# Interleaving the first loads of a fused attention block, storing its own features by unit, reordering its norm statistics, and loading its latent weights in column blocks

## The chip, the cores and the metric

The kernel runs on all 8 NeuronCores of one Trainium2 chip; the cores do not talk to each other. The metric is the device time of one execution, taken on the slowest core. Executions come in two states: in the slow one a die runs at a lower granted TensorE clock and the time is longer. Everything below compares fast executions. A profile shows one fast execution; its page is about the slowest core of that execution, so the pages of two kernels may show different cores.

## The reference, cut to what matters

```python
h = rms_norm(x, g_in)                                   # x: (2, 4096, 2048)
(c_q, c_kv, k_pe, z_mla, q_swa, k_swa, v_swa, z_swa, q_mem, z_mem) = split_cols(h @ w_in, IN_SIZES)
y_mla = mla_attention(c_q, c_kv, k_pe, ...)   # per head: q from w_uq, k and v from w_ukv; block-causal
y_swa = swa_attention(q_swa, k_swa, v_swa, ...)         # window, sinks
y_mem = memory_attention(q_mem, rms_norm(mem), ...)
y = concat([y_mla, y_swa, y_mem] * silu(gates)) @ w_out
return rms_norm(x + y, norm_final)
```

Four cores share one sequence. Each core owns 1,024 of its 4,096 tokens: it computes queries, gates and outputs for those, but compressed keys and values for all 4,096.

## The kernel before

A core's tokens come as 8 **units** of 512. Units 0 and 1 are its own tokens and stay in the buffer `hown`; units 2 to 7 pass through four rotating buffers `hrot`. Features come transposed (2,048 features in 16 chunks of 128 rows, named `kc`) as f32 in memory, and are cast to bf16 by the load; in this kernel the loads that cast go on GpSimd's queue ("pool", below the *software queue*). The weights of the units go on SyncE's queue ("sp", the *hardware queue*). For each unit TensorE forms five column groups (two of latent, one of rotary key, one of key, one of value) from the weights `wkv`. These arrive as f32 in four quarters (`wst`), and VectorE multiplies the norm gain in (*fold*) while it writes `wkv`. So a quarter of unit 0's work needs one quarter of features and one folded quarter of weights.

```python
hown = P.sb("hown", [128, 16, 1024], BF16, 34 * KB)       # [row, kc, own token]: a unit's row is cut in 1 KB runs

def load_x(i):                                            # i = half unit
    hb, ap = xhalf(i)
    n = 8 // len(hb)
    for k, b_ in enumerate(hb):
        P.dma("pool", ap[:, k * n:(k + 1) * n, :], xu_d[i]..., b_, writes=[b_])

for q in range(3):
    load_kv(q)                                            # "sp": wst[q] <- weights, f32
for i in range(4):
    load_x(i)                                             # "pool": hown <- features, f32 to bf16
...
for q in range(4):
    fold_kv(q)                                            # VectorE: wkv[q] = wst[q] * gain
    if q == 0:
        load_kv(3); load_cs(0); ...                       # first buffer free again; rotary table; identity
    ...
    stat_sq(q // 2, q % 2)                                # ScalarE: squares of the features
    for g, b in ((0, 0), (1, 1), (3, KB_), (4, VB), (2, GB)):
        group(0, g, b, 4 * q, 4 * q + 4)                  # TensorE
```

The RMS norm is applied late: ScalarE squares the features, VectorE adds the squares up (`stat_add`, into `qt`), and TensorE sums over rows with a matrix of ones (`stat_m`); the result scales what is read out of PSUM.

```python
    kpe_r(0)                          # unit 0's read-out, while TensorE is in unit 1
    kpe(0, GB)                        # three VectorE steps of the rotary key
    lat_n(0, 0)                       # two more
    stat_add(2)                       # unit 1: the first half's sum of squares
    ...
    else:                             # units 2 to 7
        ... groups 0, 1
        if u < 4: group(u, 3, KB_)
        stat_m(u)
        group(u, 2, GB)
    ...
    if u < 4:
        swa_k(u, KB_)                 # VectorE reads the key bank out
    ...
        lat_m(u, 6)
        if u > 1: group(u, 4, VB)
    if u == 3:                        # first own query product, into the key bank
        proj(wb, wp, 0, KB_)
```

After the units come the products of own tokens with streamed weights (`stage`, f32, 512 KB halves on the hardware queue; folded into `ring` by VectorE or GpSimd): query latents, memory keys and values, and 16 **gate** columns `z`. In the middle of the gates the weights of the latent stage are fetched, as two loads with a cast:

```python
        if kind == "z" and c == 3:
            P.dma("pool", wuq.t[:].rearrange("p a b -> p (a b)"), wuq_d[:, :], wuq, writes=[wuq])      # 2 MB as bf16
            P.dma("pool", wukv.t[:].rearrange("p a b -> p (a b)"), wukv_d[:, :], wukv, writes=[wukv])  # 1 MB
```

Then come the latent attention over 8 heads, and the output projection.

Of the kernel before, what the change touches and what calls it, by code (L numbers as in the profile page):

```python
# [164 lines left out]
def build():  # L165
# [32 lines left out]
    def pf(b, c0, c1, p0=0, p1=128):  # L198
        o = (b % 2) * 512
        return DB[b // 2][p0:p1, o + c0:o + c1]  # L200
# [26 lines left out]
    vv = P.sb("vv", [128, 16, 128], BF16, 30 * KB)  # L227
    hown = P.sb("hown", [128, 16, 1024], BF16, 34 * KB)
    hownp = [[P.part(hown) for _ in range(4)] for _ in range(2)]
    hrot = [P.sb("hrot", [128, 8, 512], BF16, (74 + 8 * i) * KB) for i in range(4)]  # L230
# [25 lines left out]

    def xhalf(i):

        u, kh = i // 2, i % 2
        if u < 2:  # L260
            n = len(hownp[u]) // 2
            return hownp[u][kh * n:(kh + 1) * n], hown.t[:, kh * 8:(kh + 1) * 8, u * 512:(u + 1) * 512]
        b = hrot[(i - 4) % 4]
        return [b], b.t[:, :, :]

    def hpart(u, kc):
        b, ap = xhalf(2 * u + kc // 8)
        return ap[:, kc % 8, :]

    def hbufs(u):  # L270
        return xhalf(2 * u)[0] + xhalf(2 * u + 1)[0]

    def load_x(i):
        hb, ap = xhalf(i)
        n = 8 // len(hb)
        for k, b_ in enumerate(hb):
            P.dma("pool", ap[:, k * n:(k + 1) * n, :],
                  xu_d[i].rearrange("p (a b) -> p a b", b=512)[:, k * n:(k + 1) * n, :], b_, writes=[b_])

# [3 lines left out]

    def stat_sq(i, k=None):

        hb, ap = xhalf(i)
        for j in (range(2) if k is None else (k,)):
            ks = slice(4 * j, 4 * j + 4)
            act(AF.Square, sqb.t[:, ks, :], ap[:, ks, :], [hb[j % len(hb)]], [sqp[j]])

# [14 lines left out]
    def stat_m(u):  # L305
        rb, r_, eb, e_ = r_of(u)

        def mm(e):
            for c in range(4):
                ins = e.matmul(pf(6, 0, 512), lhsT=ones.t[:], rhs=qt.t[:, c, :], start=(c == 0), stop=(c == 3))  # L310
            return ins
        P.op("pe", mm, reads=[ones, qt], writes=[PS[6]])
        act(AF.Ln, r_, pf(6, 0, 512), [PS[6]], [rb], bias=EPS, scale=1.0 / D)
        P.op("dve", lambda e: e.tensor_scalar(out=e_, in0=pf(6, 0, 512), scalar1=EPS / D, scalar2=EPS * EPS,
                                              op0=ALU.mult, op1=ALU.add), reads=[PS[6]], writes=[eb])
        act(AF.Exp, r_, r_, [rb], [rb], scale=-0.5)

    def group(u, g, b, k0=0, k1=16):


        bufs = hownp[u][k0 // 4:k1 // 4] if u < 2 else hbufs(u)

        def mm(e):
            for kc in range(k0, k1):
                if g < 4:
                    ins = e.matmul(pf(b, 0, 512), lhsT=wkv.t[:, kc, g * 128:(g + 1) * 128], rhs=hpart(u, kc),  # L326
                                   start=(kc == 0), stop=(kc == 15))
                    continue
                for t in range(4):
                    ins = e.matmul(pf(b, t * 128, (t + 1) * 128), lhsT=hpart(u, kc)[:, t * 128:(t + 1) * 128],  # L330
                                   rhs=wkv.t[:, kc, 512:640], start=(kc == 0 and t == 0), stop=(kc == 15),
                                   skip_group_check=True)
            return ins
        P.op("pe", mm, reads=wkvp[k0 // 4:k1 // 4] + bufs, writes=[PS[b]])

# [56 lines left out]

    def load_kv(q):
        w_ = wst[q % 3]
        P.dma("sp", w_.t[:].rearrange("p a b -> p (a b)"), wkv_d[q], w_, writes=[w_])

    def fold_kv(q):
        tt(ALU.mult, wkv.t[:, 4 * q:4 * q + 4, :], wst[q % 3].t[:], g_in[:, 4 * q:4 * q + 4].unsqueeze(2).to_broadcast(
            [128, 4, 640]), [wst[q % 3], gv], [wkvp[q]])

    for q in range(3):
        load_kv(q)
    for i in range(4):
        load_x(i)

# [54 lines left out]
    def proj(wb, wp, hf, b):  # L460
        def mm(e):
            for kc in range(16):
                ins = e.matmul(pf(b, 0, 512), lhsT=wb.t[:, kc, :], rhs=hown.t[:, kc, hf * 512:(hf + 1) * 512],  # L463
                               start=(kc == 0), stop=(kc == 15))
            return ins
        P.op("pe", mm, reads=wp + hownp[hf], writes=[PS[b]])
# [34 lines left out]
    for q in range(4):  # L501
        fold_kv(q)
        if q == 0:
            load_kv(3)
            load_cs(0)
            P.dma("sp", ident.t[:], idn_d[:, :], ident, writes=[ident])
        if q == 2:
            stat_add(0)
        stat_sq(q // 2, q % 2)
        for g, b in ((0, 0), (1, 1), (3, KB_), (4, VB), (2, GB)):  # L510
            group(0, g, b, 4 * q, 4 * q + 4)
            if q == 3 and g == 1:
                lat_sq(0)
    stat_add(1)
    stage.extend(P.sb("stage", [128, 8, 128], F32, (166 + 4 * i) * KB) for i in range(4))
# [3 lines left out]
    for u in (2, 3):  # L519
        load_x(2 * u)  # L520
        load_x(2 * u + 1)
        load_cs(u, "pool")
# [7 lines left out]

    stat_sq(2, 0)
    stat_m(0)
    stat_sq(2, 1)
    for q in range(2):
# [5 lines left out]
    lat_t(0, 6)  # L540
    kpe_r(0)
    kpe(0, GB)
    lat_n(0, 0)
    stat_add(2)
    stat_sq(3, 0)
    for g in range(2):
        group(1, g, 2 + g, 8, 12)
    for g, b in ((3, KB_), (4, VB), (2, GB)):
        group(1, g, b, 0, 12)
    stat_sq(3, 1)  # L550
    stat_add(3)
    load_cs(5)
    for u in range(1, 8):
        p0 = 2 * (u % 2)
        if u == 1:
            stat_m(u)
            for g in range(2):
                group(1, g, 2 + g, 12, 16)
            lat_sq(p0)
            for g, b in ((3, KB_), (4, VB), (2, GB)):  # L560
                group(1, g, b, 12, 16)
        else:
            for k in range(2):
                for g in range(2):
                    group(u, g, p0 + g, 8 * k, 8 * k + 8)
            lat_sq(p0)
            if u < 4:
                group(u, 3, KB_)
            stat_m(u)
            group(u, 2, GB)  # L570
        if u < 7:
            stat_sq(2 * u + 2)
        kpe_r(u)
# [5 lines left out]
        if u < 4:  # L579
            lat_m(u, 6)  # L580
            if u > 1:
                group(u, 4, VB)
            lat_t(u, 6)
            lat_n(u, p0)
# [19 lines left out]
        if u < 7:  # L604
            stat_sq(2 * u + 3)
            stat_add(2 * u + 3)
# [5 lines left out]
        if 1 < u < 6:  # L612
            load_x(2 * u + 4)
            load_x(2 * u + 5)
        if u == 6:
# [225 lines left out]
    for kind, c in chunks:  # L841
# [80 lines left out]
        if kind == "z" and c == 3:  # L922
            assert not side
            wuq = P.sb("wuq", [128, 4, 2048], BF16, 126 * KB)
            wukv = P.sb("wukv", [128, 2, 2048], BF16, 142 * KB)
            P.dma("pool", wuq.t[:].rearrange("p a b -> p (a b)"), wuq_d[:, :], wuq, writes=[wuq])
            P.dma("pool", wukv.t[:].rearrange("p a b -> p (a b)"), wukv_d[:, :], wukv, writes=[wukv])
            P.dma("pool", kpeT.t[64:128, :], kpeT.t[0:64, :], kpeT, reads=[kpeT], writes=[kpeT])
# [416 lines left out]
```

## Time and profile before

| | |
|---|---|
| time, median of fast runs | 820.48 us |
| TensorE busy / idle on the slowest core | 750.6 / 68.4 us |
| first matmul | 26.25 us |
| next two TensorE waits (64 and 84 us) | 3.67 and 2.47 us |
| TensorE waits among the gates (375 to 393 us) | 3.34, 0.96, 1.56 us |

The head of the page, slowest core: engine, busy time, share of the span, instructions.

```profile
span 819.0 us, 12755 instructions; the slowest of 8 cores (806.6 to 819.0 us)
...
PE 750.6 (92%) x4463; PEld 361.9 (44%) x4463; DVE 544.8 (67%) x792; ACT 424.7 (52%) x539; POOL 100.6 (12%) x82
```

TensorE waits for little, so a change can win only from its idle 68 us and from the slower matmuls after a gap (after the 3.67 us wait at 64 us, seven begin 420 to 427 ns after the one before, not 216; see below). The waits view of TensorE (line that waited, what it waited for, total us, times, longest us):

```profile
PE psd L326 <- DMA hown_57<-xu: 26.3, 1, 26.3
PE psd L310 <- DVE qt_64 L206: 6.1, 2, 3.7
PE psd L463 <- DVE zrt_114 L206: 4.9, 2, 3.3
...
PE psd L463 <- DVE zrt_113 L206: 1.0, 1, 1.0
```

The longest of them is before the first matmul. The timeline of the start shows how it comes about (columns: start, duration, engine, line, operation, output <- inputs, forms; in brackets the idle time of the engine before it and what ended it):

```profile
1.49 0.42 SPq L147 DMA_DIRECT2D wst_77<-wkv  x1
1.58 6.10 POOL L147 DMA_DIRECT2D hown_57<-xu  x8 [0.33 <-issue]
...
9.77 2.83 DVE L206 TENSOR_TENSOR wkv_62<-wst_77,gv_44 128x2560 bf16<-128x2560 f32 x1 [9.77 <-DMA wst_77<-wkv]
...
20.67 2.83 DVE L206 TENSOR_TENSOR wkv_62<-wst_79,gv_44 128x2560 bf16<-128x2560 f32 x1 [2.47 <-DMA wst_79<-wkv]
...
26.25 4.92 PE L326 MATMUL psd<-hown_57,wkv_62 128*128 128x512 bf16 x12 [26.25 <-DMA hown_57<-xu]
```

Both queues got their orders by 7.7 us. Three weight quarters land and are folded (from 9.8, 15.4 and 20.7 us on) while the first quarter of features, ordered at 1.58 us, lands only at 26.1 us. The records of DMA packets show why. In the stretch from 8 to 22 us they hold 349 weight packets of 10,240 B and 386 feature packets of 1,024 B: the counts are nearly equal, so the queue with pieces a tenth as long moved about a tenth of the other's bytes (0.40 against 3.57 MB). That the queues took turns piece by piece is inferred from the counts, since the records do not name the engine: on this core, when the first 48 feature pieces had begun, so had 31 weight pieces beyond the first quarter's 128. Spread evenly over the 16 engines, that is three pieces an engine of the one and two of the other, which long turns would not give.

The second wait, in unit 1:

```profile
56.16 1.22 DVE L206 TENSOR_TENSOR qt_64<-sqb_63 128x2048 bf16<-128x2048 bf16 x1
57.46 3.71 ACT L203 ACTIVATE sqb_63<-hown_57 128x2048 bf16<-128x2048 bf16 x2 [4.19 <-DVE qt_64 L206]
...
63.98 1.07 PE L310 MATMUL psd<-qt_64,ones_43 128*128 128x512 bf16 x4 [3.67 <-DVE qt_64 L206]
...
84.30 1.02 PE L310 MATMUL psd<-qt_64,ones_43 128*128 128x512 bf16 x4 [2.47 <-DVE qt_64 L206]
```

VectorE adds unit 1's first squares only after unit 0's rotary key and latents; ScalarE sat idle 4.19 us because the buffer of squares was not free; so the last sum was ready at 63.8 us and TensorE waited 3.67 us. The last line is the like wait in unit 2.

The waits among the gates:

```profile
376.11 1.23 DVE L206 TENSOR_TENSOR ring_87<-stage_83,gv_44 128x1024 bf16<-128x1024 f32 x1 [6.02 <-DMA stage_83<-wti]
...
378.08 8.75 PE L463 MATMUL psd<-hown_57,ring_86 128*128 128x512 bf16 x32 [3.34 <-DVE zrt_114 L206]
...
385.82 1.23 DVE L206 TENSOR_TENSOR ring_84<-stage_81,gv_44 128x1024 bf16<-128x1024 f32 x1 [4.13 <-DMA stage_81<-wti]
...
387.80 3.61 PE L463 MATMUL psd<-hown_57,ring_87 128*128 128x512 bf16 x16 [0.96 <-DVE zrt_113 L206]
...
392.97 3.61 PE L463 MATMUL psd<-hown_57,ring_87 128*128 128x512 bf16 x16 [1.56 <-DVE zrt_114 L206]
```

TensorE waits for VectorE, but VectorE had itself waited 6.02 and 4.13 us for stages, whose landing took up to 27.4 us in this stretch, beside the latent weights' pieces of 16,384 B (`wuq`) and 8,192 B (`wukv`). Note also that the 32 matmuls at 378 us took 8.75 us, about 1.7 us more than without a gap, since nine of them begin 305 to 427 ns after the one before, not 216; the trace's record of the granted clock has one half for 3.41 us from 378.84 us on. The same record has one half for 3.41 us after each of the two waits of the statistics matmul (from 64.82 and 85.30 us).

### The profile page before, as it was taken

The numbers are of one execution on the slowest core, as the hardware profiler recorded it, in microseconds if no ns is written. First come the engines' busy times: TensorE is split into PE (matmuls) and PEld (weight loads), VectorE is DVE, ScalarE is ACT, GpSimd is POOL, SyncE is SP. The second block draws the span as 40 slices with busy tenths as digits, with TensorE's granted clock in tenths as the row PEclk, the third lists the DMA queues.
The fourth block names the chain that finished last, engine by engine and source line by source line (L and its number), as shares of the span: only waits on it lengthen the run. The fifth ranks groups of instructions, "written<-read, shape, count | busy, mean of one in ns | idle before, by whom it ended". The sixth has DMA issues, their size and how long they took to land.

```text
span 819.0 us, 12755 instructions; the slowest of 8 cores (806.6 to 819.0 us)
## 1 busy us (share of the span) xinstructions
PE 750.6 (92%) x4463; PEld 361.9 (44%) x4463; DVE 544.8 (67%) x792; ACT 424.7 (52%) x539; POOL 100.6 (12%) x82
## 2 busy tenths in 40 slices
PE   0798899998789999997998999999999998999995
PEld 0353454444333454443444555545545453444442
DVE  2445676776686766764955888888888887256334
ACT  0455545554453337763545767677676775332222
POOL 5100000002232332221210110101101010000000
PEclk9999999999999999999999999999999999999998
DMA  8999489877464585489310616100101189209313
GB/s 230 196 165 218 108 168 168 172 185 197 126 155 128 147 230 144 124 153 233 103 33 0 128 30 103 28 11 17 26 2 27 35 192 217 99 1 289 122 52 103
DMA packets 24895, 99.62 MB, mean 122 GB/s; under 512 B 2750, under 2 KB 7102, under 8 KB 20544
## 3 DMA queue, kind: packets, MB, share of 16 engines
q1 hardware_dynamic: 16544, 64.58, 26.7%
q0 software_dynamic: 8288, 34.22, 25.0%
q8 instruction: 37, 0.61, 0.3%
q14 instruction: 26, 0.21, 0.1%
HBM read 115.18 MB, written 8.39 MB: 151 GB/s over the span
## 4 chain that ended last, share of the span: by engine, by line
PE 75%; DVE 11%; DMA 6%; ACT 4%; issue 4%; DVEq 0%; ACTq 0%; POOL 0%; SPq 0%; POOLq 0%
PE psd L463 19%; PE psd L1107 13%; PE psd L326 10%; PE psd L997 6%; PE psd L1029 5%; PE psd L983 4%; PE psd L831 3%; DMA hown_57<-xu 3%; DMA stage_81<-wti 3%; PE psd L817 2%; PE psd L792 2%; PE psd L330 1%; PE psd L848 1%; PE psd L310 1%; DVE pac_147 L206 1%
## 5 line engine op out<-in xcount | busy, mean ns | idle before, releaser
L463 PE MATMUL psd<-hown_57,ring_85 128*128 128x512 bf16 x288 | 64.5, 379 | 2.1 <-ACT sqq_94 L203 2.1
L326 PE MATMUL psd<-hown_57,wkv_62 128*128 128x512 bf16 x128 | 33.1, 415 | 26.3 <-DMA hown_57<-xu 26.3
L463 PE MATMUL psd<-hown_57,ring_87 128*128 128x512 bf16 x224 | 51.9, 386 | 2.5 <-DVE zrt_114 L206 1.6
L463 PE MATMUL psd<-hown_57,ring_84 128*128 128x512 bf16 x224 | 50.5, 382 | 0.0
L463 PEld LDWEIGHTS psd<-hown_57,ring_85 128*128 128x128 bf16 x288 | 27.7, 98 | 37.2 <-issue 4.6
L997 PE MATMUL psd<-Qn_122,Kb_129 128*128 128x512 bf16 (+2 forms) x192 | 43.3, 328 | 0.0
L997 PE MATMUL psd<-Qn_121,Kb_128 128*128 128x512 bf16 (+2 forms) x192 | 43.2, 328 | 0.0
L463 PE MATMUL psd<-hown_57,ring_86 128*128 128x512 bf16 x160 | 37.5, 392 | 3.3 <-DVE zrt_114 L206 3.3
L203 ACT ACTIVATE pmb_132<-psd 128x1024 bf16<-128x1024 f32 x24 | 24.6, 1024 | 26.1 <-PE psd L997 26.1
L831 PEld LDWEIGHTS psd<-wukv_120,kvnT_53 128*128 128x128 bf16 x512 | 31.5, 99 | 10.9 <-issue 7.0
L203 ACT ACTIVATE pmb_136<-psd 128x1024 bf16<-128x1024 f32 x24 | 24.5, 1021 | 22.6 <-PE psd L997 22.5
L831 PE MATMUL psd<-wukv_120,kvnT_53 128*128 128x128 bf16 x512 | 34.6, 222 | 1.4 <-ACT Kb_128 L203 1.4
L463 PEld LDWEIGHTS psd<-hown_57,ring_87 128*128 128x128 bf16 x224 | 21.8, 99 | 31.1 <-issue 6.8
L817 PE MATMUL psd<-kvnT_53,wukv_120 128*128 128x512 bf16 x128 | 33.7, 386 | 0.8 <-DVE Vb_130 L216 0.8
L463 PEld LDWEIGHTS psd<-hown_57,ring_84 128*128 128x128 bf16 x224 | 21.9, 99 | 27.3 <-issue 2.0
L326 PEld LDWEIGHTS psd<-hown_57,wkv_62 128*128 128x128 bf16 x128 | 13.1, 105 | 42.5 <-issue 31.2
L792 PE MATMUL psd<-cqT_90,wuq_119 128*128 128x512 bf16 x128 | 30.2, 379 | 0.0
L203 ACT ACTIVATE pmb_134<-psd 128x1024 bf16<-128x1024 f32 x24 | 24.6, 1024 | 7.3 <-PE psd L997 6.1
L203 ACT ACTIVATE pmb_137<-psd 128x1024 bf16<-128x1024 f32 x24 | 24.4, 1018 | 6.0 <-PE psd L997 6.0
L203 ACT ACTIVATE pmb_135<-psd 128x1024 bf16<-128x1024 f32 x24 | 24.5, 1021 | 5.4 <-PE psd L997 5.4
L463 PEld LDWEIGHTS psd<-hown_57,ring_86 128*128 128x128 bf16 x160 | 16.0, 100 | 23.7 <-issue 6.1
L203 ACT ACTIVATE r2t_72<-r2t_72 128x512 f32<-128x512 f32 x16 | 10.1, 630 | 29.5 <-DVE r2t_72 L209 28.7
(402 smaller groups left out, 1649.0 us busy)
## 6 DMA issues: line engine op xcount, KB each, us to landing
stage_82<-wti SPq DMA_DIRECT2D x15, 512.0 KB, 7.2
stage_83<-wti SPq DMA_DIRECT2D x15, 512.0 KB, 6.6
stage_80<-wti SPq DMA_DIRECT2D x11, 512.0 KB, 6.6
stage_81<-wti SPq DMA_DIRECT2D x11, 512.0 KB, 6.3
hown_57<-xu POOLq DMA_DIRECT2D x8, 512.0 KB, 33.6
tq_151<-tq_126 SPq DMA_DIRECT2D x14, 256.0 KB, 3.4
hrot_58<-xu POOLq DMA_DIRECT2D x3, 1024.0 KB, 11.1
hrot_59<-xu POOLq DMA_DIRECT2D x3, 1024.0 KB, 18.8
```

The costliest lines, as they stand in the source:

```text
L203: P.op("act", lambda e: e.activation(out=out, in_=in_, func=func, **kw), reads=reads, writes=writes)
L206: P.op(eng, lambda e: e.tensor_tensor(out=out, in0=a, in1=b, op=op), reads=reads, writes=writes)
L310: ins = e.matmul(pf(6, 0, 512), lhsT=ones.t[:], rhs=qt.t[:, c, :], start=(c == 0), stop=(c == 3))
L326: ins = e.matmul(pf(b, 0, 512), lhsT=wkv.t[:, kc, g * 128:(g + 1) * 128], rhs=hpart(u, kc), start=(kc == 0), stop=(kc == 15))
L463: ins = e.matmul(pf(b, 0, 512), lhsT=wb.t[:, kc, :], rhs=hown.t[:, kc, hf * 512:(hf + 1) * 512], start=(kc == 0), stop=(kc == 15))
L792: ins = e.matmul(pf(2 * k + hf, 0, 512), lhsT=wuq.t[:, kc, col:col + 128], rhs=cqT.t[:, kc, hf * 512:(hf + 1) * 512], start=(kc == 0), sto ...
L817: ins = e.matmul(pf(2 * k + t, 0, 512), lhsT=wukv.t[:, kc, h * 256:h * 256 + 128], rhs=kvnT.t[:, kc, (2 * c + t) * 512:(2 * c + t + 1) * 512],
L831: ins = e.matmul(pf(2 * k + t // 4, (t % 4) * 128, (t % 4 + 1) * 128), lhsT=kvnT.t[:, kc, tl * 128:(tl + 1) * 128], rhs=wukv.t[:, kc, h * ...
L983: ins = e.matmul(pf(2 * k + t, c0, c1), lhsT=kpeT.t[rows, tile * 128:(tile + 1) * 128], rhs=Qp[s].t[rows, q0 + qc:q0 + qc + c1 - c0], star ...
L997: ins = e.matmul(pf(2 * k + t, c0, c1), lhsT=Kb[s].t[:, tile * 128:(tile + 1) * 128], rhs=Qn[s].t[:, q0 + qc:q0 + qc + c1 - c0], start=Fal ...
L1029: ins = e.matmul(pf(ob, qc, qc + c1 - c0), lhsT=Vb[s].t[:, tile, :], rhs=pb.t[:, t, c0:c1], start=(st["first"] and i == 0), stop=(lst and ...
L1107: ins = e.matmul(pf(b, 0, 512), lhsT=gate(kc)[:, tt_ * 128:(tt_ + 1) * 128], rhs=wo[ci].t[:, kc, :], start=(kc == 0), stop=(kc == 15))
```

## The change

It has four parts. (1) Weight quarters 1 to 3 move to the software queue, alternating with the quarters of unit 0's features, in order of use; weight quarter 0 stays on the hardware queue, and the rotary table and the identity now follow it at once; the last feature quarter is cut in two. (2) `hown` is stored by unit, so that a feature quarter is one 4 KB run per row instead of four of 1 KB. (3) The order of statistics and latent-norm steps in units 0 to 3 changes. (4) The latent weights come in blocks of 512 columns: eight loads of 1 KB runs instead of one of 16 KB runs (`wuq`) and one of 8 KB runs (`wukv`).

```diff
-    hown = P.sb("hown", [128, 16, 1024], BF16, 34 * KB)
+    hown = P.sb("hown", [128, 2, 16, 512], BF16, 34 * KB)
+    cuts = [(0, 4, 8, 12, 14, 16), (0, 4, 8, 12, 16)]
 ...
+    load_kv(0, "sp")
+    load_cs(0)
+    P.dma("sp", ident.t[:], idn_d[:, :], ident, writes=[ident])
     for q in range(3):
-        load_kv(q)
-    for i in range(4):
-        load_x(i)
+        load_xk(0, 4 * q, 4 * q + 4)
+        if q < 2:
+            load_kv(q + 1)                # now on "pool"
 ...
         if q == 0:
             load_kv(3)
-            load_cs(0)
-            P.dma("sp", ident.t[:], idn_d[:, :], ident, writes=[ident])
+            load_xk(0, 12, 14)
+            load_xk(0, 14, 16)
+            load_x(1)
 ...
     kpe_r(0)
+    stat_add(2)
     kpe(0, GB)
     lat_n(0, 0)
-    stat_add(2)
 ...
             if u < 4:
                 group(u, 3, KB_)
-            stat_m(u)
-            group(u, 2, GB)
+                group(u, 2, GB)
+                stat_m(u)
+            else:
+                stat_m(u)
+                group(u, 2, GB)
 ...
-            lat_m(u, 6)
             if u > 1:
                 group(u, 4, VB)
+            lat_m(u, 6)
 ...
-            P.dma("pool", wuq.t[:]..., wuq_d[:, :], wuq, writes=[wuq])
-            P.dma("pool", wukv.t[:]..., wukv_d[:, :], wukv, writes=[wukv])
+            for w_, d_ in ((wuq, wuq_d), (wukv, wukv_d)):
+                for c_ in range(4):
+                    cs_ = slice(c_ * 512, (c_ + 1) * 512)
+                    P.dma("pool", w_.t[:, :, cs_], d_.rearrange("p (a b) -> p a b", b=2048)[:, :, cs_], w_, writes=[w_])
```

Besides, unit 0's squares are summed in another way (four more ones-matmuls instead of a VectorE addition), and the squares of unit 1's first quarter are taken after unit 0's statistics matmul.

More of the change, by code (lines that the diff above doesn't have):

```diff
@@ L227, in build @@
     vv = P.sb("vv", [128, 16, 128], BF16, 30 * KB)
-    hown = P.sb("hown", [128, 16, 1024], BF16, 34 * KB)
-    hownp = [[P.part(hown) for _ in range(4)] for _ in range(2)]
+    hown = P.sb("hown", [128, 2, 16, 512], BF16, 34 * KB)
+    cuts = [(0, 4, 8, 12, 14, 16), (0, 4, 8, 12, 16)]
+    hownp = [[P.part(hown) for _ in c_[1:]] for c_ in cuts]
     hrot = [P.sb("hrot", [128, 8, 512], BF16, (74 + 8 * i) * KB) for i in range(4)]
@@ L255, in build, with fparts, feats, load_xk @@
     OUTS = [P.mk(None), P.mk(None)]
-    def xhalf(i):
-        u, kh = i // 2, i % 2
+    def fparts(u, k0, k1):
         if u < 2:
-            n = len(hownp[u]) // 2
-            return hownp[u][kh * n:(kh + 1) * n], hown.t[:, kh * 8:(kh + 1) * 8, u * 512:(u + 1) * 512]
-        b = hrot[(i - 4) % 4]
-        return [b], b.t[:, :, :]
-    def hpart(u, kc):
-        b, ap = xhalf(2 * u + kc // 8)
-        return ap[:, kc % 8, :]
-    def hbufs(u):
-        return xhalf(2 * u)[0] + xhalf(2 * u + 1)[0]
-    def load_x(i):
-        hb, ap = xhalf(i)
-        n = 8 // len(hb)
-        for k, b_ in enumerate(hb):
-            P.dma("pool", ap[:, k * n:(k + 1) * n, :],
-                  xu_d[i].rearrange("p (a b) -> p a b", b=512)[:, k * n:(k + 1) * n, :], b_, writes=[b_])
+            return [b_ for b_, c0, c1 in zip(hownp[u], cuts[u], cuts[u][1:]) if c0 < k1 and k0 < c1]
+        return [hrot[(2 * u + kh) % 4] for kh in range(2) if 8 * kh < k1 and k0 < 8 * kh + 8]
+    def feats(u, k0, k1):
+        if u < 2:
+            return hown.t[:, u, k0:k1, :]
+        return hrot[(2 * u + k0 // 8) % 4].t[:, k0 % 8:k0 % 8 + k1 - k0, :]
+    def hpart(u, kc):
+        return feats(u, kc, kc + 1)[:, 0, :]
+    def load_xk(u, k0, k1):
+        (b_,) = fparts(u, k0, k1)
+        i, j = 2 * u + k0 // 8, (k0 % 8) * 512
+        P.dma("pool", feats(u, k0, k1).rearrange("p a b -> p (a b)"), xu_d[i][:, j:j + (k1 - k0) * 512], b_, writes=[b_])
+    def load_x(u):
+        for k0, k1 in zip(cuts[u], cuts[u][1:]) if u < 2 else ((0, 8), (8, 16)):
+            load_xk(u, k0, k1)
     def load_cs(u, q="sp"):
@@ L282, in load_cs, with stat_sq @@
         P.dma(q, c_.t[:], csk_d[u], c_, writes=[c_])
-    def stat_sq(i, k=None):
-        hb, ap = xhalf(i)
-        for j in (range(2) if k is None else (k,)):
-            ks = slice(4 * j, 4 * j + 4)
-            act(AF.Square, sqb.t[:, ks, :], ap[:, ks, :], [hb[j % len(hb)]], [sqp[j]])
+    def stat_sq(u, k0, k1):
+        for a0 in range(k0, k1, min(4, k1 - k0)):
+            a1 = min(a0 + 4, k1)
+            act(AF.Square, sqb.t[:, a0 % 8:a0 % 8 + a1 - a0, :], feats(u, a0, a1), fparts(u, a0, a1), [sqp[a0 % 8 // 4]])
     def stat_add(i):
@@ L306, in stat_m @@
         rb, r_, eb, e_ = r_of(u)
+        parts = [qt.t[:, c, :] for c in range(4)] + ([sqb.t[:, c, :] for c in range(4, 8)] if u == 0 else [])
         def mm(e):
-            for c in range(4):
-                ins = e.matmul(pf(6, 0, 512), lhsT=ones.t[:], rhs=qt.t[:, c, :], start=(c == 0), stop=(c == 3))
+            for i, a_ in enumerate(parts):
+                ins = e.matmul(pf(6, 0, 512), lhsT=ones.t[:], rhs=a_, start=(i == 0), stop=(i == len(parts) - 1))
             return ins
-        P.op("pe", mm, reads=[ones, qt], writes=[PS[6]])
+        P.op("pe", mm, reads=[ones, qt] + ([sqp[1]] if u == 0 else []), writes=[PS[6]])
         act(AF.Ln, r_, pf(6, 0, 512), [PS[6]], [rb], bias=EPS, scale=1.0 / D)
@@ L318, in group @@
     def group(u, g, b, k0=0, k1=16):
-        bufs = hownp[u][k0 // 4:k1 // 4] if u < 2 else hbufs(u)
+        bufs = fparts(u, k0, k1)
         def mm(e):
@@ L333, in mm @@
             return ins
-        P.op("pe", mm, reads=wkvp[k0 // 4:k1 // 4] + bufs, writes=[PS[b]])
+        P.op("pe", mm, reads=wkvp[k0 // 4:(k1 + 3) // 4] + bufs, writes=[PS[b]])
     def lat_sq(p0):
@@ L391, in build, with load_kv @@
     wst = [P.sb("wst", [128, 4, 640], F32, (166 + 10 * i) * KB) for i in range(3)]
-    def load_kv(q):
+    def load_kv(q, eng="pool"):
         w_ = wst[q % 3]
-        P.dma("sp", w_.t[:].rearrange("p a b -> p (a b)"), wkv_d[q], w_, writes=[w_])
+        P.dma(eng, w_.t[:].rearrange("p a b -> p (a b)"), wkv_d[q], w_, writes=[w_])
     def fold_kv(q):
@@ L462, in mm @@
             for kc in range(16):
-                ins = e.matmul(pf(b, 0, 512), lhsT=wb.t[:, kc, :], rhs=hown.t[:, kc, hf * 512:(hf + 1) * 512],
+                ins = e.matmul(pf(b, 0, 512), lhsT=wb.t[:, kc, :], rhs=hown.t[:, hf, kc, :],
                                start=(kc == 0), stop=(kc == 15))
@@ L504, in build @@
             load_kv(3)
-            load_cs(0)
-            P.dma("sp", ident.t[:], idn_d[:, :], ident, writes=[ident])
+            load_xk(0, 12, 14)
+            load_xk(0, 14, 16)
+            load_x(1)
         if q == 2:
-            stat_add(0)
-        stat_sq(q // 2, q % 2)
-        for g, b in ((0, 0), (1, 1), (3, KB_), (4, VB), (2, GB)):
-            group(0, g, b, 4 * q, 4 * q + 4)
-            if q == 3 and g == 1:
-                lat_sq(0)
-    stat_add(1)
+            tt(ALU.add, qt.t[:], sqb.t[:, 0:4, :], sqb.t[:, 4:8, :], sqp, [qt])
+        if q == 3:
+            tt(ALU.add, qt.t[:], qt.t[:], sqb.t[:, 0:4, :], [qt, sqp[0]], [qt])
+        for k0, k1 in ((4 * q, 4 * q + 4),) if q < 3 else ((12, 14), (14, 16)):
+            stat_sq(0, k0, k1)
+            for g, b in ((0, 0), (1, 1), (3, KB_), (4, VB), (2, GB)):
+                group(0, g, b, k0, k1)
+                if k1 == 16 and g == 1:
+                    lat_sq(0)
     stage.extend(P.sb("stage", [128, 8, 128], F32, (166 + 4 * i) * KB) for i in range(4))
@@ L519, in build @@
     for u in (2, 3):
-        load_x(2 * u)
-        load_x(2 * u + 1)
+        load_x(u)
         load_cs(u, "pool")
@@ L529, in build @@
     P.dma("pool", sel.t[:], sel_d[:, :], sel, writes=[sel])
-    stat_sq(2, 0)
     stat_m(0)
-    stat_sq(2, 1)
+    stat_sq(1, 0, 8)
     for q in range(2):
@@ L541, in build @@
     kpe_r(0)
+    stat_add(2)
     kpe(0, GB)
     lat_n(0, 0)
-    stat_add(2)
-    stat_sq(3, 0)
+    stat_sq(1, 8, 12)
     for g in range(2):
@@ L549, in build @@
         group(1, g, b, 0, 12)
-    stat_sq(3, 1)
+    stat_sq(1, 12, 16)
     stat_add(3)
@@ L568, in build @@
                 group(u, 3, KB_)
-            stat_m(u)
-            group(u, 2, GB)
+                group(u, 2, GB)
[3 more added lines that the diff above has]
+                group(u, 2, GB)
         if u < 7:
-            stat_sq(2 * u + 2)
+            stat_sq(u + 1, 0, 8)
         kpe_r(u)
@@ L604, in build @@
         if u < 7:
-            stat_sq(2 * u + 3)
+            stat_sq(u + 1, 8, 16)
             stat_add(2 * u + 3)
@@ L612, in build @@
         if 1 < u < 6:
-            load_x(2 * u + 4)
-            load_x(2 * u + 5)
+            load_x(u + 2)
         if u == 6:
@@ L925, in build @@
             wukv = P.sb("wukv", [128, 2, 2048], BF16, 142 * KB)
-            P.dma("pool", wuq.t[:].rearrange("p a b -> p (a b)"), wuq_d[:, :], wuq, writes=[wuq])
-            P.dma("pool", wukv.t[:].rearrange("p a b -> p (a b)"), wukv_d[:, :], wukv, writes=[wukv])
+            for w_, d_ in ((wuq, wuq_d), (wukv, wukv_d)):
+                for c_ in range(4):
+                    cs_ = slice(c_ * 512, (c_ + 1) * 512)
+                    P.dma("pool", w_.t[:, :, cs_], d_.rearrange("p (a b) -> p a b", b=2048)[:, :, cs_], w_, writes=[w_])
             P.dma("pool", kpeT.t[64:128, :], kpeT.t[0:64, :], kpeT, reads=[kpeT], writes=[kpeT])
```

## The prediction

> **What bounds the kernel.** The page has TensorE busy 750.6 of 819.0 us on the slowest core, so its idle 68 us are what can be won. The waits view puts 26.3 us into the first matmul's wait for the first quarter of own features, and 6.1 us into two waits of the statistics matmul for VectorE (3.7 at 64 us, 2.5 at 84 us). The timeline at 360 to 400 us has three TensorE waits of 3.3, 1.0 and 1.6 us for VectorE, which had itself waited 6.0 and 4.1 us for weight stages. Other waits are untouched. After a gap matmuls run at 427 ns instead of 216 for a while (12 took 4.92 us, not 2.6): about 1.7 us each time. [...]
>
> **Start.** The packet records show the two queues served descriptor by descriptor in turn: weights in 10,240 B pieces against features in 1,024 B pieces. So three f32 weight quarters (landed 9.6, 15.3, 20.6 us) overtook the first feature quarter (26.1). [...] The change puts them in one queue in order of use, features in 4 KB pieces. At 305 GB/s of f32 read (feature quarter 3.4 us, weight quarter 4 us), estimated landings: weights and features 0 about 10, then 14.3/17.8, 22/25.4, 29.5/32.9; unit 1's at 36 to 47. With a 2.8 us fold, quarters begin on TensorE at about 13, 18.5, 25.5 and 32.5 us; unit 0 ends at about 37 (before 45.8). The start becomes load-bound, with gaps between quarters and the half-clock restarts hidden in them. Total bytes are unchanged, so unit 1's last feature comes only 2 to 3 us earlier (49.7 before).
>
> **Units 1 to 3.** The sum moved ahead of the rotary-key work lets the squares start earlier: the 3.7 us wait goes. Statistics after the fourth group remove the 2.5 us one. Each restart saved is 1.7 us. Added: 4 ones-matmuls (0.9 us), two half squares. Second halves landing near 61 and 75 us may cost 1 us. Unit 3 ends at 96 to 98 instead of 113.15: 15 to 17 us. Units 4 to 7 are TensorE-bound (18.6 us each, no wait), their loads released by TensorE, so this carries through.
>
> **Latent weights.** From 16,384 B descriptors (1.5 to 1.9 us each) to 1,024 B, against 4,096 B stage descriptors (0.3 us). Stages should land in 8 to 10 us instead of 20, so the three waits and a restart mostly vanish: 5 to 7 us. The latents take an estimated 35 us instead of 25, but are needed about 60 us after issue.
>
> **Sum.** 820.5 - 16 - 6 = 798 us; range 791 to 806. Faster 0.88, same 0.11, slower 0.01.
>
> **Signs.** First matmul at 12 to 15 us, released by the fold; quarters separated by waits on DMA or fold; no VectorE waits of the statistics matmul at units 1 and 2; unit 4's first group at 103 to 106 instead of 120; no TensorE wait over 1 us among the gates' columns; attention and output merely shifted.
>
> **What would make it wrong.** Software-queue startup (first feature packet at 7.8 us before) delaying everything; the fourth weight quarter, which waits for a fold, draining the queue; VectorE or ScalarE becoming the limit in unit 1 (margin under 1 us); latent weights starved; gains given back at a later wait.

The traces of the kernel before have what the terms use: the 12 matmuls from 26.25 us on are up to 427 ns apart, and after the waits at 64 and 84 us the clock record has one half for 3.41 us each, of which half, 1.7 us, is lost; that the queues were served in turn is inferred from the counts (349 to 386); from 355 to 380 us pieces of 16,384 B took 1.71 us in the mean, pieces of 4,096 B 0.27. The 305 GB/s is an estimate; the packets from 8 to 22 us hold 4.36 MB counted as f32 read, which is 0.31 MB per us.

## The result, and the profile after

The changed kernel takes **799.5 us** (median of its four fast runs, 798.46 to 800.36) against 820.48. The ratio is 0.9744 (95% interval 0.9725 to 0.9762). Ratios here and below are the mean time of one kernel's fast runs over that of the other's fast runs of the same rounds, so not quite the ratio of the medians quoted.

The head of the page, and TensorE's waits, of the slowest core (this time core 5):

```profile
span 796.9 us, 12778 instructions; the slowest of 8 cores (793.1 to 796.9 us)
...
PE 748.5 (94%) x4467; PEld 361.9 (45%) x4467; DVE 542.3 (68%) x791; ACT 424.8 (53%) x540; POOL 105.4 (13%) x92
```

```profile
PE psd L327 <- DMA hown_57<-xu: 14.8, 1, 14.8
PE psd L327 <- DVE wkv_62 L206: 5.2, 2, 2.7
...
PE psd L467 <- DVE kT_55 L206: 1.5, 1, 1.5
```

The wait for the first matmul fell from 26.3 to 14.8 us, but two waits for the fold (5.2 us together) came; both waits of the statistics matmul and all three among the gates are gone; a wait of 1.5 us for `kT`, the key read-out, is new. The other cores agree on the statistics and on `kT`; among the gates core 2 still has a wait of 1.46 us (at 369.53 us) and core 3 one of 0.47. The start in the timeline:

```profile
10.41 2.83 DVE L206 TENSOR_TENSOR wkv_62<-wst_77,gv_44 128x2560 bf16<-128x2560 f32 x1 [10.41 <-DMA wst_77<-wkv]
13.80 0.53 POOL L147 DMA_DIRECT2D wst_77<-wkv  x1 [9.43 <-DVE wkv_62 L206]
...
14.83 5.28 PE L327 MATMUL psd<-hown_57,wkv_62 128*128 128x512 bf16 x12 [14.83 <-DMA hown_57<-xu]
...
28.88 2.75 PE L327 MATMUL psd<-hown_57,wkv_62 128*128 128x512 bf16 x12 [2.50 <-DVE wkv_62 L206]
...
33.01 2.82 DVE L206 TENSOR_TENSOR wkv_62<-wst_77,gv_44 128x2560 bf16<-128x2560 f32 x1 [3.25 <-DMA wst_77<-wkv]
...
36.09 1.49 PE L327 MATMUL psd<-hown_57,wkv_62 128*128 128x512 bf16 x6 [2.70 <-DVE wkv_62 L206]
```

TensorE begins at 14.83 us, released by the feature quarter; the folded weights had been ready since 13.24 us (10.41 + 2.83). The last weight quarter, ordered at 13.80 us behind all that was in the queue, is folded from 33.01 us on, and the last quarter of unit 0 starts at 36.09 us. What such a gap costs differs: the one of 2.50 us up to 28.88 us was not followed by half clock here (12 matmuls in 2.75 us), nor was one of 2.94 us at the same place on core 1, but one of 2.42 us on core 2 was (the clock record has one half from 30.22 us on, for 3.41 us; matmuls 427 ns apart). So the length of a gap alone did not decide it. Unit 1:

```profile
49.50 1.22 DVE L206 TENSOR_TENSOR qt_64<-sqb_63 128x2048 bf16<-128x2048 bf16 x1
...
50.80 3.71 ACT L203 ACTIVATE sqb_63<-hown_57 128x2048 bf16<-128x2048 bf16 x2 [0.38 <-DVE qt_64 L206]
...
57.32 1.02 PE L311 MATMUL psd<-qt_64,ones_43 128*128 128x512 bf16 x4
```

The sum `qt` now runs at 49.50 us, the squares follow at 50.80, and the statistics matmul at 57.32 us waits for nothing. The gates, and the new wait in unit 3:

```profile
368.58 7.07 PE L467 MATMUL psd<-hown_57,ring_87 128*128 128x512 bf16 x32
...
375.49 7.07 PE L467 MATMUL psd<-hown_57,ring_84 128*128 128x512 bf16 x32
```

```profile
101.14 0.69 DVE L206 TENSOR_TENSOR kT_55<-psd,rot_70 128x512 bf16<-128x512 f32 x1
...
101.98 7.07 PE L467 MATMUL psd<-hown_57,ring_84 128*128 128x512 bf16 x32 [1.50 <-DVE kT_55 L206]
```

The 32-matmul blocks follow each other without a gap (368.58, 375.49 us: every 6.91 us). In unit 3, the key bank is read out (`kT`) only after the late statistics (whose matmul starts at 95.45 us), and the own-query product which wants that bank waits 1.50 us.

To place the gain, take the starts of certain matmuls from the instruction records of each kernel's profiled run, averaged over the eight cores (us). *Unit 0 ends* is the start of its statistics matmul.

| stretch | before | after | gain |
|---|---|---|---|
| start, to the first matmul | 25.69 | 13.74 | 11.95 |
| start, to unit 0's end | 44.98 | 39.96 | 5.02 |
| unit 0's end to unit 3's own-query product | 67.02 | 60.01 | 7.01 |
| from there to the first gate | 181.60 | 181.12 | 0.48 |
| first gate to first product with latent weights | 120.78 | 114.30 | 6.48 |
| from there to the end | 400.70 | 399.90 | 0.80 |
| whole | 815.08 | 795.29 | 19.79 |

So 12 us of the first matmul's wait are won, but only 5 us remain when unit 0 is done. The largest piece is in units 1 to 3, where the reordering is.

### The profile page after: what moved, and what is told of

Its sections match the earlier page's. It is cut to its first block, busy times and chain, and to the rows that moved or that the text cites. A ratio compares the mean times of both kernels' runs of the same rounds, so it can differ in the third digit from the quotient of the medians.

```text
span 796.9 us, 12778 instructions; the slowest of 8 cores (793.1 to 796.9 us)
## 1 busy us (share of the span) xinstructions
PE 748.5 (94%) x4467; PEld 361.9 (45%) x4467; DVE 542.3 (68%) x791; ACT 424.8 (53%) x540; POOL 105.4 (13%) x92
## 4 chain that ended last, share of the span: by engine, by line
PE 81%; DVE 8%; ACT 4%; DMA 3%; issue 3%; DVEq 0%; ACTq 0%; SPq 0%; POOLq 0%
PE psd L467 23%; PE psd L1116 14%; PE psd L327 11%; PE psd L1006 7%; PE psd L1038 6%; PE psd L992 4%; PE psd L838 4%; DMA wst_77<-wkv 3%; PE psd L824 2%; PE psd L799 2%; PE psd L331 1%; PE psd L311 1%; DVE pac_147 L206 1%; DVE wkv_62 L206 1%; PE psd L869 1%
## 5 line engine op out<-in xcount | busy, mean ns | idle before, releaser
L327 PE MATMUL psd<-hown_57,wkv_62 128*128 128x512 bf16 x128 | 33.6, 414 | 20.0 <-DMA hown_57<-xu 14.8
L467 PEld LDWEIGHTS psd<-hown_57,ring_85 128*128 128x128 bf16 x288 | 27.7, 98 | 37.2 <-issue 4.6
L838 PEld LDWEIGHTS psd<-wukv_120,kvnT_53 128*128 128x128 bf16 x512 | 31.5, 99 | 10.8 <-issue 6.9
L467 PEld LDWEIGHTS psd<-hown_57,ring_87 128*128 128x128 bf16 x224 | 22.1, 100 | 28.8 <-issue 4.4
L467 PEld LDWEIGHTS psd<-hown_57,ring_84 128*128 128x128 bf16 x224 | 21.7, 98 | 28.6 <-issue 2.9
L327 PEld LDWEIGHTS psd<-hown_57,wkv_62 128*128 128x128 bf16 x128 | 12.8, 104 | 36.3 <-issue 25.7
L992 PE MATMUL psd<-Qp_124,kpeT_54 64*128 64x512 bf16 (+2 forms) x192 | 23.5, 326 | 2.1 <-ACT pmb_137 L203 1.3
L206 POOL TENSOR_TENSOR Qp_124<-tq_126,tq_151 128x1024 bf16<-128x1024 f32 x4 | 9.4, 2348 | 118.6 <-DMA tq_151<-tq_126 87.7
```

What stands on the lines that cost most here:

```text
L206: P.op(eng, lambda e: e.tensor_tensor(out=out, in0=a, in1=b, op=op), reads=reads, writes=writes)
L327: ins = e.matmul(pf(b, 0, 512), lhsT=wkv.t[:, kc, g * 128:(g + 1) * 128], rhs=hpart(u, kc), start=(kc == 0), stop=(kc == 15))
L467: ins = e.matmul(pf(b, 0, 512), lhsT=wb.t[:, kc, :], rhs=hown.t[:, hf, kc, :], start=(kc == 0), stop=(kc == 15))
L838: ins = e.matmul(pf(2 * k + t // 4, (t % 4) * 128, (t % 4 + 1) * 128), lhsT=kvnT.t[:, kc, tl * 128:(tl + 1) * 128], rhs=wukv.t[:, kc, h * ...
L992: ins = e.matmul(pf(2 * k + t, c0, c1), lhsT=kpeT.t[rows, tile * 128:(tile + 1) * 128], rhs=Qp[s].t[rows, q0 + qc:q0 + qc + c1 - c0], star ...
```

## The experiments

Twelve kernels ran; all gave correct results. The kernel before was run again (medians 819.24, 817.96 and 817.80 us, each on another chip). It drifts by up to 2.7 us, so absolute times are compared only where the difference is larger than that; for the rest there are the stretches inside the profiles. The starts quoted are means over eight cores, as in the table above.

### e1: the latents whole again

```diff
-            for w_, d_ in ((wuq, wuq_d), (wukv, wukv_d)):   # 8 blocks of columns
-                ...
+            P.dma("pool", wuq.t[:]..., wuq_d[:, :], wuq, writes=[wuq])
+            P.dma("pool", wukv.t[:]..., wukv_d[:, :], wukv, writes=[wukv])
```

> The change without its last part: latent weights again as two whole loads. Theory (the latents' large descriptors starved the weight stages; worth about 6.5 us of the 19.8): time about 806.5 us, 6 to 8 us over the changed kernel, with TensorE waits of about 3, 1 and 1.5 us among the gates' columns back, and stage loads of about 20 us. Rival (the gain among the gates came from the earlier start, which moved the stages out of step with the latents): no such waits, about 800 us.

Measured: 805.76 us (805.34 to 806.31), ratio to before 0.9841 (0.9823 to 0.9860). First gate to first latent product takes 120.56 us, against 114.30 with the blocks and 120.78 before. The timeline of the gates has the waits back, with VectorE's wait for a stage ahead of them:

```profile
362.51 1.23 DVE L206 TENSOR_TENSOR ring<-stage,gv 128x1024 bf16<-128x1024 f32 x1 [5.27 <-DMA stage<-wti]
...
364.49 8.75 PE L467 MATMUL psd<-hown,ring 128*128 128x512 bf16 x32 [2.60 <-DVE zrt L206]
...
374.78 3.40 PE L467 MATMUL psd<-hown,ring 128*128 128x512 bf16 x15 [1.54 <-DVE zrt L206]
```

The theory holds and the rival falls: the earlier start did nothing for the gates.

### e2: the latents in blocks, nothing else

```diff
 (the kernel before)
-            P.dma("pool", wuq...), P.dma("pool", wukv...)
+            the eight blocks of columns
```

> The kernel before with the latents in column blocks and nothing else. If the parts add up: about 814 us (6 to 7 us under before), TensorE at the first latent product 6 to 7 us earlier relative to the first memory product, start as before (first matmul 25 to 26 us). If the start and this part interact: outside 812 to 816.

Measured: 813.76 us median, ratio 0.9925 (0.9886 to 0.9964); one of its four runs was slow and is left out. First gate to first latent product is 114.51 us; the start is that of before (first matmul 25.01 us). The part is independent of the others, and worth 6 us.

### e3: the layout alone, two queues as before

```diff
 (the kernel before)
-    hown = P.sb("hown", [128, 16, 1024], BF16, 34 * KB)
+    hown = P.sb("hown", [128, 2, 16, 512], BF16, 34 * KB)
-        P.dma("pool", ap[:, k * n:(k + 1) * n, :], ...)          # four runs of 1 KB per row
+        P.dma("pool", ap[...].rearrange("p a b -> p (a b)"), ...)  # one run of 4 KB per row
```

> The kernel before with own features stored by unit (4 KB descriptors in place of 1 KB), still two queues. Theory A (the two queues are served descriptor by descriptor, so 1 KB against 10 KB is what starved the features): feature quarter 0 lands at about 16 us instead of 26, in step with weight quarter 1; first matmul 16 to 17 us, unit 0 ends at 40 to 41 us against 45.0 before and 40.0 after, so the layout alone does most of what the queue order does at the start; time about 816 us. Theory B (only the order in one queue helps): first matmul stays at 23 us or later, time about 820.

Measured: 815.09 us median of four fast runs (one was slow), ratio 0.9951 (0.9927 to 0.9974). The first matmul starts at 16.52 us and unit 0 ends at 40.14 us; the first feature quarter lands at 16.4 us (mean), together with weight quarter 1 at 17.3. The DMA view of 8 to 24 us (queue: packets, MB, share of the 16 engines' time), first before, then with the layout alone (q1 is the hardware queue with the weights, q0 the software queue with the features; small packets of 4 B are counted too, 55 of the 461):

```profile
q1 hardware_dynamic: 461, 4.03, 74.5%
q0 software_dynamic: 450, 0.46, 25.9%
```

```profile
q1 hardware_dynamic: 321, 2.84, 54.3%
q0 software_dynamic: 320, 1.18, 47.9%
```

```profile
15.87 4.61 PE L326 MATMUL psd<-hown,wkv 128*128 128x512 bf16 x12 [15.87 <-DMA hown<-xu]
```

By the counts the two queues still take turns about packet for packet (461 to 450, and 321 to 320), but a feature piece is four times as long, so 1.18 MB instead of 0.46 pass. Theory A holds: the length of the pieces is what starved the features. The 3.67 us wait in unit 1 is untouched, as it should be.

### e4: the old layout, one queue

```diff
 (the changed kernel)
-    hown = P.sb("hown", [128, 2, 16, 512], BF16, 34 * KB)
+    hown = P.sb("hown", [128, 16, 1024], BF16, 34 * KB)
```

> The changed kernel with own features stored as before (1 KB descriptors), still one queue. Theory A (descriptor size matters only against another queue's descriptors): first matmul 14 to 15 us, unit 0 ends at 40 to 41.5 us, time 800 to 801.5 us. Theory B (small descriptors are slow in themselves): landings stretch by more than 2 us at unit 0's end, time 803 us or more.

Measured: 800.28 us median, ratio 0.9783 (0.9754 to 0.9813); first matmul 14.15 us. In one queue there is nobody to take turns with, and pieces of 1 KB do no visible harm (unit 0 ends at 39.90 us, with 4 KB at 39.96). (The ratio is 0.4% above the changed kernel's, with intervals that overlap; unit 0 ends at the same time.) So either cure is enough for the start:

| | first matmul | unit 0 ends |
|---|---|---|
| before | 25.69 | 44.98 |
| layout alone (e3) | 16.52 | 40.14 |
| one queue, old layout (e4) | 14.15 | 39.90 |
| both (the change) | 13.74 | 39.96 |

### e5: the statistics in the old order

```diff
 (the changed kernel)
     kpe_r(0)
-    stat_add(2)
     kpe(0, GB)
     lat_n(0, 0)
+    stat_add(2)
 ...
-                group(u, 2, GB)
-                stat_m(u)
-            else:
-                stat_m(u)
-                group(u, 2, GB)
+            stat_m(u)
+            group(u, 2, GB)
 ...
+            lat_m(u, 6)
             if u > 1:
                 group(u, 4, VB)
-            lat_m(u, 6)
```

> The changed kernel with the statistics and latent-norm steps of units 0 to 3 back in the old order. Theory (the reordering is worth more than the earlier start: 8.7 of the 13.7 us won by unit 3's start came after unit 0): TensorE waits of about 3.7 and 2.5 us for the sum of squares are back, statistics of unit 2 about 4 us and unit 3's start about 7 us later relative to unit 0's end, the 1.5 us wait in unit 3 gone; time 805 to 808 us. Rival (the waits had been caused by late features, so the earlier loads remove them whatever the order): time within 2 us of 800.

Measured: 807.51 us median of three fast runs (one was slow), ratio 0.9874 (0.9858 to 0.9890). Unit 0 ends at 40.20 us as in the changed kernel, unit 3's own-query product starts at 107.53 instead of 99.97. TensorE's timeline on the slowest core:

```profile
58.68 1.87 PE L311 MATMUL psd<-qt,ones 128*128 128x512 bf16 x4 [3.67 <-DVE qt L206]
...
79.68 1.02 PE L311 MATMUL psd<-qt,ones 128*128 128x512 bf16 x4 [2.07 <-DVE qt L206]
```

Both waits for the sum of squares are back, although features come as early as in the changed kernel. So those waits came from the order of the work on VectorE and ScalarE, not from late features. The time lies in the range that I had set, and the rival's (within 2 us of 800) is excluded.

### e6: the statistics of unit 3 early

```diff
 (the changed kernel)
             if u < 4:
                 group(u, 3, KB_)
+            if u == 2:
                 group(u, 2, GB)
                 stat_m(u)
```

> The changed kernel with the statistics matmul of unit 3 alone put back ahead of its last group. Theory (the late statistics of unit 3 hold up the eviction of its key bank, which the first own-query product needs at once: the new 1.5 us wait for the key eviction): the wait goes, unit 4 starts about 1.5 us earlier, time 798.5 us. Rival (VectorE is behind for another reason): wait stays, time 800.

Measured: 798.18 us median of five fast runs, ratio 0.9759 (0.9746 to 0.9772). Unit 4 starts at 105.98 us instead of 106.88: 0.9 us, not 1.5. Of these, 0.3 us were already there at unit 0's end (39.63 against 39.96 us), before anything that this edit changes; from there on 0.6 us is won. The timeline of the slowest core:

```profile
91.00 1.02 PE L311 MATMUL psd<-qt,ones 128*128 128x512 bf16 x4 [0.93 <-DVE qt L206]
...
97.95 0.69 DVE L206 TENSOR_TENSOR kT<-psd,rot 128x512 bf16<-128x512 f32 x1
...
99.31 6.85 PE L467 MATMUL psd<-hown,ring 128*128 128x512 bf16 x31
```

The key bank is read out (from 97.95 us) before the own-query product needs it (99.31), which waits no more. But the statistics matmul now waits 0.93 us for its sum, so part is given back: 1.50 less 0.93 is the 0.6 us.

### e7: the latents in blocks of rows

```diff
 (the changed kernel)
-                for c_ in range(4): ... w_.t[:, :, 512 columns]      # 8 loads, runs of 1 KB
+                for c_ in range(n_): ... w_.t[:, c_, :]              # 6 loads, runs of 4 KB
```

> The changed kernel with the latents in six loads of 4 KB descriptors (one per row block) in place of eight of 1 KB. Theory (what counts is a latent descriptor's length against a stage descriptor's 4 KB, served in turn): stages share about half the engines' time and land in 10 to 12 us; part of the waits is back, time 800.5 to 803.5 us. Rival (what counts is that the load is split into several DMAs): as good as the changed kernel, 800 us.

Measured: 803.57 us median, ratio 0.9821 (0.9802 to 0.9839), just above the range that the theory allowed. First gate to first latent product takes 116.72 us: 2.4 us more than with 1 KB pieces, about 4 less than whole. On the slowest core one wait is back:

```profile
375.92 1.23 DVE L206 TENSOR_TENSOR ring<-stage,gv 128x1024 bf16<-128x1024 f32 x1 [4.73 <-DMA stage<-wti]
...
377.89 7.46 PE L467 MATMUL psd<-hown,ring 128*128 128x512 bf16 x26 [2.41 <-DVE zrt L206]
```

Cutting into several loads is not enough; how much was won went with the length of the pieces here (114.30 us with 1 KB, 116.72 with 4 KB, 120.56 with 16 and 8 KB).

### e8: weight quarter 0 in the software queue as well

```diff
 (the changed kernel)
-    load_kv(0, "sp")
-    load_cs(0)                      # tables: now issued after the loop, still on "sp"
     for q in range(3):
         load_xk(0, 4 * q, 4 * q + 4)
+        if q == 0:
+            load_kv(0)
```

> The changed kernel with weight quarter 0 also in the software queue, behind feature quarter 0, so that the other queue holds only small tables. Theory (the software queue's first data come about 6 us after its first issue, whatever else runs): first feature packet still at 7 to 8 us, feature quarter 0 landed at about 12, weight quarter 0 at about 16, first matmul at 19 us, unit 0 ends about 4 us later, time 803 to 805 us. Rival (weight quarter 0 in the other queue held the first feature packets back): first feature packet at 4 to 5 us, first matmul by 15 us.

My theory fell here. In all eight cores the first feature packet came at 3.6 to 4.0 us, where it had come at 7.0 to 8.3 us in the changed kernel. The DMA view from 3 to 7 us, first of the changed kernel (one queue only is at work), then of this one:

```profile
q1 hardware_dynamic: 84, 0.86, 87.0%
```

```profile
q0 software_dynamic: 73, 0.30, 65.6%
q1 hardware_dynamic: 173, 0.26, 32.7%
```

So the queue does not need six microseconds to start (its first packet came about 2.2 us after its first order, at 3.8 against 1.57 us); it had been held back by weight quarter 0 in the other queue. The rival's second forecast failed: the first matmul did not come by 15 us, since weight quarter 0 is now behind the features.

And yet unit 0 ends at 40.33 us, 0.4 us from the changed kernel, and the single run took 798.84 us, not the 803 to 805 that I had set. When TensorE starts, 13.7 or 17.5 us, makes no difference to when unit 0 is done.

### e9: the tables later

```diff
 (the changed kernel)
     load_kv(0, "sp")
-    load_cs(0)
-    P.dma("sp", ident.t[:], ...)
 ...
-            load_x(1)
+            load_xk(1, 0, 4)
+            load_xk(1, 4, 8)
+            load_cs(0, "pool")
+            P.dma("pool", ident.t[:], ...)
+            load_xk(1, 8, 12)
+            load_xk(1, 12, 16)
```

> The changed kernel with 0.32 MB of tables taken from the head of the loads to a place behind the second quarter of unit 1's features. Theory (unit 0's end is set by the bytes ahead of its last quarter, at about 0.31 MB per us): the fourth quarters land and unit 0 ends about 1 us earlier, unit 4 starts about 1 us earlier, time about 799. Rival (something else, as fold or TensorE, sets unit 0's end): no shift over 0.3 us.

Measured: 798.52 us median of five fast runs, ratio 0.9766 (0.9752 to 0.9779). Unit 0 ends at 38.74 us, 1.2 us earlier, for 0.32 MB less ahead of it (at 0.31 MB per us that is 1.0). So the bytes ahead set it. Unit 4 starts only 0.5 us earlier. TensorE's timeline on the slowest core shows where the rest went:

```profile
45.38 4.48 PE L327 MATMUL psd<-hown,wkv 128*128 128x512 bf16 x20 [1.55 <-DMA hown<-xu]
```

At 45.38 us unit 1 now waits 1.55 us for its own features, which lie behind the same bytes.

### e10: both

```diff
 (the changed kernel)
+            if u == 2:                      # e6: statistics of unit 3 early
 ...
-    load_cs(0)                              # e9: tables behind unit 1's second quarter
-    P.dma("sp", ident.t[:], ...)
+            load_cs(0, "pool")
+            P.dma("pool", ident.t[:], ...)
```

> The changed kernel with the tables later and the statistics of unit 3 early. If both gains stand and add: 797 to 798 us, the fastest so far. If the wait they remove comes back elsewhere: 798 to 800.

Measured: 798.43 us median of five fast runs, ratio 0.9763 (0.9748 to 0.9777); unit 4 starts at 105.99 us, as in e6 alone (105.98). The gains do not add. All of e6, e9 and e10 have lower medians than the changed kernel's 799.5 us, but they ran in other calls, in which the kernel before was also faster, and their ratios to it (0.9759 to 0.9766) are no lower than the changed kernel's (0.9744, interval to 0.9762). That one of them beats the changed kernel is not shown.

### e11: weight quarter 0 in two transfers

```diff
 (the changed kernel, load_kv; pieces of 10,240 B become two times 5,120 B)
-        P.dma(eng, w_.t[:]..., wkv_d[q], w_, writes=[w_])
+        for c_ in range(2) if eng == "sp" else (None,):
+            ...
+            P.dma(eng, w_.t[:, ks, :]..., wkv_d[q][:, cs_], w_, writes=[w_])
```

> The changed kernel with weight quarter 0, the one in the other queue, loaded as two transfers of 5,120 B descriptors. With it in the other queue whole, the first feature packet came at 7.0 to 8.3 us in every run; with it away, at 3.6 to 4.0. Theory A (one transfer's descriptors, once taken, are finished first): first feature packet at about 5.5 us. Theory B (all that lies in the other queue at that time goes first, whatever its cut): still 7 to 8 us. Either way unit 0's end, set by bytes, moves under 0.5 us and the time stays near 799.

Measured: one run of 799.70 us; the first feature packet came at 4.8 to 6.0 us on the eight cores, 5.5 in the mean. From 3 to 7 us:

```profile
q1 hardware_dynamic: 141, 0.64, 64.5%
q0 software_dynamic: 47, 0.19, 30.8%
```

Theory A holds: the first feature packet came when the hardware queue's first transfer was nearly through, at 7.7 us in the mean in the changed kernel (115 to 123 of its 128 weight pieces had begun by then on the eight cores), at 5.5 with that transfer halved, and at 3.6 to 4.0 without it (e8). (Whether it is the transfer or a number of pieces that counts is not separated: half a quarter has 128 pieces just as the whole one has, only shorter.) Unit 0 ends at 40.30 us, as expected, although the first matmul comes only at 16.69 us.

### e12: the order of statistics alone

```diff
 (the kernel before)
     kpe_r(0)
+    stat_add(2)
     kpe(0, GB)
     lat_n(0, 0)
-    stat_add(2)
 ...
-            stat_m(u)
-            group(u, 2, GB)
+                group(u, 2, GB)
+                stat_m(u)
+            else:
+                stat_m(u)
+                group(u, 2, GB)
 ...
-            lat_m(u, 6)
             if u > 1:
                 group(u, 4, VB)
+            lat_m(u, 6)
```

> The kernel before with only the new order of statistics and latent-norm steps in units 0 to 3, loads and layouts as before. Theory (this part is independent of the loads and the largest of the three): the 3.7 and 2.5 us waits go, unit 4 starts 7 us earlier, time 811.5 to 813.5 us. Rival (it needs the earlier loads: unit 2's features land too late otherwise): gain under 4 us, new TensorE waits for features of units 2 and 3.

Measured: 811.43 us median of three fast runs (two were slow), ratio 0.9915 (0.9899 to 0.9932). Unit 4 starts at 110.80 us instead of 118.85, with the first matmul still at 25.20 us, and no TensorE wait for the features of units 2 and 3 appears; the new wait of 1.5 us for `kT` does, on all cores, so it comes with this part. The part is worth 7 to 8 us by itself, with no load touched.

The three parts alone give, by their ratios, 0.5% (e3), 0.75% (e2) and 0.85% (e12): together 2.1%, of the 2.6% that the change gives. With intervals of 0.2 to 0.4% on each, the parts add up as far as can be told.

## Why the prediction was right, and where it was off

The time was 1.5 us above the forecast of 798, within the range, and the direction and the three places of the gain were right. Point by point:

- **Start: over-estimated, 9 us forecast against 5 measured.** The forecast had unit 0 end at 37 us instead of 45.8; it ended at 40.0 instead of 45.0 (means; on the slowest cores, 42.1 instead of 45.8). The term that was mis-sized is "weights and features 0 about 10". Features 0 landed at 13.6 us in the mean. From there on the forecast was good: the last piece of unit 0's features landed 22.6 us later (36.15), where 22.9 was forecast (10 to 32.9). From 2.5 us on, the two quarters' 2.36 MB at my 0.305 MB per us give 10.2 us; I had left out the tables, which make it 11.3, and taken a rate from a later stretch for the head of the loads, where it is lower. On core 5 the packets from 2.5 to 13.6 us carried 0.26 MB per us (counted as f32 read), those from 13.6 to 36 us 0.32. Why the head is slower stays open.
- **"The start becomes load-bound": right, and shown.** e8 starts TensorE 3.8 us later and ends unit 0 within 0.4 us of the same time; e9 takes 0.32 MB away and ends it 1.2 us earlier. For that reason the software queue's start, which I had listed as the first risk, is not the cause of the missing 4 us: in e8 its first packet came 3.9 us earlier and unit 0 ended no earlier.
- **Released "by the fold": wrong on six of the eight cores,** the slowest among them, where it was the features; on cores 3 and 7 the fold ended last, 0.11 and 0.02 us after the features had landed.
- **Units 1 to 3: right in size, 7.2 us forecast (16 less the 8.8 of unit 0) against 7.0.** Both waits and their half-clock restarts went: before, the clock record has one half after the wait at 64 us on all eight cores and after that at 84 us on seven; after, it has none between 41 and 125 us. As an estimate, 3.67 + 2.47 us of waits and twice 1.7 us for 3.41 us at half clock are 9.5 us; less the new wait of 1.5 us that is 8.0, and e12 measured 7.9 from unit 0's end to unit 3's own-query product. The changed kernel also runs four more ones-matmuls there (0.86 us), which leaves 7.2. e12 gives this gain without any change of loads, and e5 takes it away with all other parts in place, so this is the reordering's doing. That the size came out is in part luck: the forecast allowed 1 us for late features, for which TensorE never waited in these units, and did not have the new wait of 1.5 us, in unit 3: its late statistics hold up the read-out of the bank that the next product writes. e6 removes it and, after a new wait of 0.93 us, gets 0.6 us back.
- **"Unit 4's first group at 103 to 106 instead of 120": missed** on the slowest core (108.9 us), and in the mean (106.9), by the sizes above, the start's above all.
- **Latents: right, 5 to 7 us forecast, 6.5 measured;** e1, e2 and e7 show the cause. The stage loads took longer than the 8 to 10 us of the forecast: 9.8 to 15.8 us for those touched from 336 to 372 us on core 5, against up to 27.4 in the same stretch of before. On core 5 that was still soon enough: VectorE did not wait for them. On six of the other seven cores it did (longest 0.5 to 4.2 us), and on core 2 TensorE with it for 1.46 us, so "no TensorE wait over 1 us among the gates' columns" held on seven cores. The price was paid by the latents: on core 5 the last of them landed 47 us after the first order (341 to 388 us), not the 35 forecast; the first product with them starts at 395 us in the mean, so the margin is thin.
- **"Attention and output merely shifted": right,** 400.7 against 399.9 us.

## What to carry to other kernels

When two queues are busy at once, look at the length of their pieces before their order: by the counts the engines took turns piece by piece here (386 to 349), so a load with 1 KB runs next to one with 10 KB runs moved about a tenth of its bytes (0.40 against 3.57 MB), and storing its target so that it arrives in longer runs cured the start as well as moving everything into one queue did (unit 0 ends at 40.14 and 39.90 us); the same lever, turned the other way, let a background load yield to the stream that the engines wait for (first gate to first latent product 114.30 us instead of 120.56). An earlier first matmul was not as much of an earlier finish (12 us became 5 by unit 0's end): ask what bounds the stage's end, here the bytes ahead of its last quarter (0.32 MB less, 1.2 us earlier, in e9). And a small reordering, mostly of VectorE steps, which touched no load, was worth as much as either change of loads (0.85% against 0.5 and 0.75); after such a move, check which bank is read out later than before.
